# A two-layer encoder on one core: later block ends, later memory keys, and four more row-tile pairs in seven products

## The chip, the cores and the metric

The kernel runs on one core of a Trainium2 chip. The metric is the device time of one execution in microseconds; the time of a kernel is the median of its runs. The profile is one further execution under the hardware profiler. Engines are named as there: PE is the matrix engine (PEld its weight loads), DVE the vector engine, ACT the scalar engine, POOL the GpSimd engine, and SP the engine that issues most DMAs.

## What is computed

An encoder of two layers on one sequence of 256 tokens, model width 2048, all in float32:

```python
for l in range(DEPTH):                       # 2
    h = rmsnorm(x, norm_g[l])
    proj = h @ w_in[l]                       # 2048 x 7168: a_x a_b a_c a_g | d_q d_k d_v d_g | m_q m_g
    y_a = short_gated_conv(a_x, a_b, a_c, conv_w[l], conv_b[l]) * silu(a_g)        # 768 wide
    q, k = rmsnorm(d_q), rmsnorm(d_k)        # 6 heads x 2 halves x 64
    o_d = softmax(q1 k1 + alibi) v - lam * softmax(q2 k2 + alibi) v
    y_d = rmsnorm(o_d, g) * (1 - lam_init) * silu(d_g)                             # 768 wide
    mk, mv = split(rmsnorm(mem, mem_norm_g[l]) @ w_mem_kv[l])                      # 256 memory tokens
    y_m = softmax(rmsnorm(m_q) rmsnorm(mk)) mv * silu(m_g)                         # 512 wide, 4 heads
    x = x + concat(y_a, y_d, y_m) @ w_out[l]
```

## The kernel before, and what orders its work

**Products in three parts.** A float32 operand is split in two numbers, hi and lo: ACT rounds it (`hi`), DVE subtracts (`lo`). A product is three matmuls, hi x hi, hi x lo and lo x hi, each 128x512 (`products`, L278, and `product`, L325). Activations stand turned (features on partitions) as stationary tiles: `xT` for the input of a layer, `yT` for the mixed heads, `memT` for the memory. Weights stream: a chunk is two row tiles (256 rows) of 512 columns, loaded by SP into one of four `raw` buffers, split into one of four `hi` and one of four `lo` buffers (`load_w`, L263). 256 tokens are two token tiles, so a chunk is 2 x 2 x 3 = 12 matmuls.

**Blocks.** `block` (L286) makes 512 columns of a projection: eight chunks into two PSUM accumulators (there are four `acc` banks, so two blocks' worth). Layer 0 goes first through the memory's keys and values of both layers, then blocks 0 to 5 of the attention columns (0 to 2 are queries and keys, 3 to 5 values and gates), then the memory head's two blocks, then the convolution's six, then the output projection.

**Pairs in seven products.** Two neighbouring column blocks (near and far) and two row tiles make a 2x2 by 2x2 product, which `seven` (L345) computes with seven products in place of eight: the weights come in as two `wide` tiles of 1024 columns, DVE forms four differences, ACT and DVE split them; sums of the token tiles come from `token_sums` (L330). `joint` (L1033) runs a near block with some of its row tiles as pairs: it opens the far block's accumulators and four more banks `x1, x5, x6, x7`; the keys of `places` say before which row index a pair is emitted, `collect` adds the x banks up into `u`, and `gather` (L1066) adds the block's accumulators to them. Before, one pair is made in layer 0 (blocks 3 and 4, before index 10) and one in layer 1 (blocks 1 and 2, before index 8), besides those of the output projections.

**Ends of blocks.** After its last chunk a block's accumulators are read. For queries and keys that is `normed_steps` (L405): ACT squares groups of 64 columns with a sum (L413), POOL turns the sums into row factors (L414, L185, an ALU power), ACT multiplies each group by its factor (L421) into a sheet; then `qk_T` (L500) turns the sheet: a DVE transpose of 32x32 blocks (L451), a trip through DRAM (`carry`, L468 and L472, on SP) and a split into `yT`. Before, `normed` runs all of `normed_steps` at once, directly behind the block. Other ends are read by ACT and DVE in place: gates by `silu2`, values by a scaled copy, the convolution's inputs by `scaled`, `times` and `gate`.

**Memory keys.** `mem_keys` (L809) norms a layer's keys in the same way (groups of 128), and `keys` (L815) turns them: four DMAs out and one back on POOL's queue (L821, L822, `kd`), then a DVE transpose into `mkT` (L824), held in program order.

**What sets the order.** The program is written as one sequence with side tasks: `run_side` (L208) counts chunks and runs one step of each task that is due; `later(g, n)` (L191) makes a task due n chunks on, and a task's `yield n` puts its next step n chunks later. A scheduler then orders each engine's instructions by their readiness in its own estimate, except those wrapped in `keep_in_program_order` (`pin`), which keep the order in which they were emitted. Each engine works through its queue in order, so an instruction that waits holds up all behind it.

Of the kernel before, what the change touches and what calls it, by code (L numbers as in the profile page):

```python
# [40 lines left out]
BIG = 3.0e38  # L41

# [7 lines left out]
def encoder(ctx: ExitStack, tc: tile.TileContext, x, mem, norm_g, w_in, conv_w, conv_b,  # L50
# [354 lines left out]
    def normed_steps(acc, gs, st, home):  # L405

        ng, w = NB // gs, gs // B
        ss = small.tile([P, NT, ng], F32, tag=f"ss{ng}", name=nm("ss"))
        r = small.tile([P, NT, ng], F32, tag=f"rs{ng}", name=nm("rs"))
        for t in range(NT):  # L410
            for g in range(ng):
                sq = small.tile([P, gs], F32, tag="sq", name=nm("sq"), bufs=1)
                nc.scalar.activation(sq, acc[t][:, g * gs:(g + 1) * gs], AF.Square, accum_out=ss[:, t, g:g + 1])  # L413
            nc.gpsimd.tensor_scalar(ss[:, t], ss[:, t], 1.0 / gs, col(st, ET, t), ALU.mult, ALU.add)  # L414
            rsqrt(r[:, t], ss[:, t])
            yield 1
        both = home()
        for t in range(NT):
            for g in range(ng):
                j, b = divmod(g * w, NA)  # L420
                nc.scalar.activation(both[:, b:b + w, j, t], strips(acc[t][:, g * gs:(g + 1) * gs]), AF.Copy,  # L421
                                     scale=r[:, t, g:g + 1])
# [233 lines left out]

    def mem_pair(l, n, st):
        heads = (2 * n, 2 * n + 1)
        es = []
        for h in heads:  # L660
            while held["e"] == 2:
                yield 1
            held["e"] += 1
            es.append((yield from mem_scores(l, h, st)))
            yield 2
        yield 4
# [142 lines left out]
    def mem_keys(l, kraw):  # L809

        nat = yield from normed_steps([kraw[:, t] for t in range(NT)], P, stm[0], sheets("v"))
        yield 6
        yield from keys(l, nat)

    def keys(l, nat):  # L815


        d = dram.tile([NA, B, NA, W_MEM // P * NT * B], F32, name=nm("kd"))
        flat = nat.rearrange("p b j t c -> p b (j t c)")
        for a in range(NA):  # L820
            tc.keep_in_program_order(nc.gpsimd.dma_start(d[:, :, a].rearrange("b c r -> c b r"), flat[a * B:(a + 1) * B]))  # L821
        tc.keep_in_program_order(nc.gpsimd.dma_start(flat, d.rearrange("b c a r -> (b c) a r")))  # L822
        yield 8
        tc.keep_in_program_order(nc.vector.transpose(  # L824
            mkT[l].rearrange("p j (t a i) -> p (j t) a i", t=NT, a=NA),
            nat.rearrange("p a j t c -> p (j t) a c")))
# [5 lines left out]
    class Memory:  # L832
# [5 lines left out]
        def load(self, s):  # L838
            if s in self.raw or s in self.parts or s >= DEPTH * KT + KT // CK:
                return  # L840
            l, k = divmod(s, KT)
            self.raw[s] = raw_tile()
            if l == DEPTH:
                pin(nc.sync.dma_start(self.raw[s], x_row_tiles(w_in[0], k * CK)[:, :, C_D:C_D + NB]))
# [170 lines left out]
    for l in range(DEPTH):  # L1015
# [11 lines left out]
        def x_sums(n, tag):  # L1027
            home = keep.tile([P, 2, 4, P], F32R, tag=tag, name=nm("sums"))
            for _ in token_sums(xT, 2 * n, home):
                pass  # L1030
            return home

        def joint(b, places, summed, home):  # L1033
# [18 lines left out]
            def pair_at(n):  # L1052
                def run(near):
                    rows = lambda k: x_row_tiles(w_in[l], k, 1)[:, 0, C_D + b * NB:C_D + (b + 2) * NB]
                    seven(xT, 2 * n, summed[n], rows, near, far, x, n == 0, n == len(places) - 1,
                          ((tmp, ("sh", "e")[n]),) * 2, lambda: None, ((tmp, "e"), (keep, "mga"))[l])
# [6 lines left out]
                    between={c: pair_at(n) for n, c in enumerate(places)})  # L1063
# [13 lines left out]
        near_b, far_b, places, tags, home = ((3, 4, (10,), ("bgx",), "bgT"), (1, 2, (8,), ("bgT",), "bgx"))[l]  # L1077
        far, summed = None, []
        for b in order:
            if l == 0 and b == near_b - 1:  # L1080
                summed = [x_sums(n, tags[n]) for n in range(len(places))]
            if b in begun:
                acc = x_block([(C_D + b * NB, NB)], ALLK[-QT:], acc=begun[b])
                if b == 3:
                    for n in range(len(places)):
                        summed.append(x_sums(n, tags[n]))
            elif b == near_b:
                acc, far, us = joint(b, places, summed, home)
                acc = gather(acc, us[0:2])
            elif b == far_b:  # L1090
                acc = x_block([(C_D + b * NB, NB)], ALLK[2 * len(places):], acc=far, opened=(True, False))
                acc = gather(acc, us[2:4])
            else:
                acc = x_block([(C_D + b * NB, NB)], ready=m.ready if l == 0 and b == order[0] else None)
# [10 lines left out]
            if b < 3:  # L1105
                tasks.append(later(qk_T(l, yT, normed(acc, HALF, st, sheets(("mqT", "mga", "e")[b])),
                                 (0, 0, 4) if b == 0 else (0, 4, 2) if b == 1 else None,
                                 (256, 0, 2) if b == 1 else (0, 2, 4) if b == 2 else None), 8))
            else:
                for t in range(NT):  # L1110
                    if b == 3:
                        nc.scalar.activation(v[:, t, 0:NB], acc[t], AF.Copy, scale=col(st, R, t))
                    elif b == 4:
                        nc.scalar.activation(v[:, t, NB:768], acc[t][:, 0:256], AF.Copy, scale=col(st, R, t))
                        silu2(ga[:, t, 0:256], acc[t][:, 256:512], st, t)
                    else:
                        silu2(ga[:, t, 256:768], acc[t], st, t)
# [5 lines left out]
        def turn_mq(nat):  # L1123
# [4 lines left out]
        tasks.append(later(turn_mq(normed(acc, P, st, sheets("bgx"))), 8))  # L1128
        acc = x_block([(C_M + W_MEM, NB)])
        for t in range(NT):  # L1130
            a = tmp.tile([P, NB], F32, tag="nat", name=nm("a"), bufs=3)
            silu2(a, acc[t], st, t)
            tc.keep_in_program_order(nc.vector.transpose(mga[:, :, :, t], a.rearrange("p (j b c) -> p b j c", b=NA, c=B)))
# [62 lines left out]
        acc = x_block([(C_B, NB)])  # L1196
        scaled(both_rows(bg, 0, 4), acc, HR2)
        acc = x_block([(C_B + NB, 256), (C_G + NB, 256)])
        scaled(both_rows(bg, 4, 6), [a[:, 0:256] for a in acc], HR2)
        gate(NB, 256, [a[:, 256:512] for a in acc])  # L1200
        acc = x_block([(C_G, NB)])
        gate(0, NB, acc)
        tasks.append(later(turn_bg(list(range(CG))), 9))
        acc = x_block([(C_X, NB)])
        ux = sheet(tmp, "e")
        scaled(both_rows(ux, 0, 4), acc, R2)
        acc = x_block([(C_C, NB)])
        times(both_rows(ux, 0, 4), acc)
# [12 lines left out]
        acc = x_block([(C_X + NB, 256), (C_C + NB, 256)])  # L1221
        ux = sheet(tmp, "yn", 2)
        scaled(both_rows(ux, 0, 2), [a[:, 0:256] for a in acc], R2)
        times(both_rows(ux, 0, 2), [a[:, 256:512] for a in acc])
        tasks.append(later(conv([4, 5], ux, wait=3), 4))
# [110 lines left out]
```

## Time and profile before

| | us |
|---|---|
| median of 3 runs (lowest, highest) | 918.17 (917.14, 918.65) |
| profiled execution | 920.46 |
| span of its instructions | 918.7 |
| PE busy | 910.9 |
| DVE busy | 638.8 |
| ACT busy | 589.0 |
| POOL busy | 125.3 |

The granted clock of PE was 1.0 of full speed. In the rows that follow, a group of instructions reads: line, engine, operation, output<-inputs (buffer numbers left out), shape, count, then busy us and mean ns, then the idle time of the engine before them and what ended it. A timeline row reads: start us, duration us, engine, line, operation; in brackets the idle time before it and its releaser. Line numbers are those of the kernel before.

### The profile page before, as it was taken

What the parts mean: (1) busy time and instruction counts of PE and PEld (TensorE: products, weight loads), DVE (VectorE), ACT (ScalarE), POOL (GpSimd) and SP (SyncE); (2) the same over time, 40 slices, a digit from 0 to 9 for tenths busy, and PEclk for the clock granted to TensorE, in tenths of its full rate; (3) what the DMA queues carried; (4) which work ended last, traced back from release to release, by engine and by line L of the source; (5) the groups of instructions that cost most, each with busy time, mean ns of one, the idle gap of its engine ahead of it and who ended that gap; (6) DMA issues with size and microseconds to landing.
All of it is one profiled execution on the core that took longest, in us unless ns stands there. A gap on an engine that the chain in (4) does not pass through costs nothing.

```text
span 918.7 us, 12662 instructions
## 1 busy us (share of the span) xinstructions
PE 910.9 (99%) x4203; PEld 752.3 (82%) x4203; DVE 638.8 (70%) x877; ACT 589.0 (64%) x1226; POOL 125.3 (14%) x187
## 2 busy tenths in 40 slices
PE   9999999999999999999999999999999999999998
PEld 6887787888888888888888888888888888888887
DVE  5557645677658658677689666667658678588786
ACT  6679776757767656545557558787667666546352
POOL 2376142200031010000000202221032010000000
PEclk9999999999999999999999999999999999999999
DMA  8898777876777989978776874988768998968842
GB/s 288 284 266 252 236 227 226 255 215 221 222 212 205 256 228 262 265 234 246 254 228 226 259 251 130 277 241 238 223 183 230 266 271 248 271 206 241 281 154 92
DMA packets 244051, 215.18 MB, mean 234 GB/s; under 512 B 131977, under 2 KB 171721, under 8 KB 243985
## 3 DMA queue, kind: packets, MB, share of 16 engines
q1 hardware_dynamic: 239008, 208.71, 76.1%
q0 software_dynamic: 3776, 4.59, 1.9%
q10 hardware_dynamic: 1200, 1.07, 0.3%
q8 instruction: 33, 0.54, 0.2%
q14 instruction: 34, 0.27, 0.1%
HBM read 193.30 MB, written 21.00 MB: 233 GB/s over the span
## 4 chain that ended last, share of the span: by engine, by line
PE 88%; DMA 5%; ACT 2%; DVE 2%; POOL 2%; issue 1%; DVEq 0%; ACTq 0%; POOLq 0%
PE acc L282 80%; PE x L328 2%; DMA raw<-in_w_mem_kv_dram 2%; DMA raw<-in_w_in_dram 2%; PE acc L328 2%; PE po L489 1%; PE s L579 1%; DMA sh<-kd 1%; DVE lo L869 1%; PE po L706 1%; DVE xf L743 1%; ACT hi L271 1%; ACT sq L413 1%; POOL rs L185 1%; ACT sh L421 0%
## 5 line engine op out<-in xcount | busy, mean ns | idle before, releaser
L282 PE MATMUL acc<-hi,xT 128*128 128x512 f32 x1760 | 550.4, 390 | 0.0
L272 DVE TENSOR_TENSOR lo<-raw,hi 128x1024 fp32r<-128x1024 f32 x266 | 323.6, 1221 | 171.0 <-ACT hi L271 166.1
L271 ACT CAST hi<-raw 128x1024 fp32r<-128x1024 f32 x266 | 278.4, 1052 | 189.0 <-PE acc L282 138.2
L282 PEld LDWEIGHTS acc<-hi,xT 128*128 128x128 f32 x1760 | 330.3, 188 | 68.6
L282 PE MATMUL acc<-lo,xT 128*128 128x512 f32 x880 | 343.1, 390 | 2.0 <-DVE lo L272 1.6
L282 PEld LDWEIGHTS acc<-lo,xT 128*128 128x128 f32 x880 | 165.2, 188 | 36.3 <-DVE lo L272 2.0
L282 PE MATMUL acc<-hi,yT 128*128 128x512 f32 (+1 forms) x432 | 134.2, 388 | 0.0
L282 PEld LDWEIGHTS acc<-hi,yT 128*128 128x128 f32 x432 | 81.0, 188 | 16.7
L282 PE MATMUL acc<-lo,yT 128*128 128x512 f32 x216 | 83.7, 388 | 0.0
L282 PE MATMUL acc<-hi,memT 128*128 128x512 f32 x248 | 78.7, 393 | 0.0
L869 DVE SCALAR_TENSOR_TENSOR lo<-raw,cva,hi 128x1024 fp32r<-128x1024 f32 (+1 forms) x34 | 40.7, 1218 | 24.8 <-ACT hi L868 24.8
L282 PEld LDWEIGHTS acc<-hi,memT 128*128 128x128 f32 x248 | 46.1, 188 | 9.5
L282 PE MATMUL acc<-lo,memT 128*128 128x512 f32 x124 | 48.6, 392 | 0.7 <-DVE lo L869 0.7
L282 PEld LDWEIGHTS acc<-lo,yT 128*128 128x128 f32 x216 | 40.6, 188 | 8.4
L868 ACT ACTIVATE hi<-raw,cva 128x1024 fp32r<-128x1024 f32 (+1 forms) x34 | 36.5, 1098 | 7.6 <-DMA raw<-in_w_mem_kv_dram 7.0
L354 ACT CAST hi<-wide 128x1024 fp32r<-128x1024 f32 x21 | 22.0, 1056 | 18.1 <-DVE wide L357 7.4
L185 POOL TENSOR_TENSOR rs<-ss,root 128x8 f32<-128x8 f32 (+1 forms) x20 | 31.7, 1583 | 1.7
L354 DVE TENSOR_TENSOR lo<-wide,hi 128x1024 fp32r<-128x1024 f32 x21 | 25.4, 1221 | 8.4 <-ACT hi L354 8.2
L414 POOL TENSOR_SCALAR ss<-ss,st 128x8 f32<-128x8 f32 (+1 forms) x16 | 10.5, 654 | 137.4 <-ACT sq L413 137.4
L282 PEld LDWEIGHTS acc<-lo,memT 128*128 128x128 f32 x124 | 23.3, 188 | 6.6 <-DVE lo L869 1.8
L596 ACT ACTIVATE e<-e,mx 128x256 f32<-128x256 f32 x48 | 23.8, 497 | 6.7 <-DVE mx L591 6.0
L394 POOL TENSOR_SCALAR stt<-ssum 128x2 f32<-128x2 f32 x3 | 1.5, 507 | 187.3 <-DVE ssum L770 187.3
(207 smaller groups left out, 858.6 us busy)
## 6 DMA issues: line engine op xcount, KB each, us to landing
raw<-in_w_in_dram SPq DMA_DIRECT2D x188, 512.0 KB, 4.9
raw<-in_w_out_dram SPq DMA_DIRECT2D x54, 512.0 KB, 4.6
raw<-in_w_in_dram SPq DMA_DIRECT2D x64, 256.0 KB, 4.1
raw<-in_w_mem_kv_dram SPq DMA_DIRECT2D x30, 512.0 KB, 6.1
d<-sh SPq DMA_DIRECT2D x88, 128.0 KB, 4.4
sh<-d SPq DMA_DIRECT2D x72, 128.0 KB, 3.8
wide<-in_w_out_dram SPq DMA_DIRECT2D x10, 512.0 KB, 5.9
xs<-in_x_dram SPq DMA_DIRECT2D x4, 512.0 KB, 6.5
```

Of the source, the lines that this page charges most:

```text
L185: nc.gpsimd.tensor_tensor(r, t, root[:, 0:n], ALU.pow)
L271: nc.scalar.copy(hi, raw)
L272: nc.vector.tensor_tensor(lo_, raw, hi.bitcast(F32), ALU.subtract)
L282: i = nc.tensor.matmul(acc, left, right, start=start, stop=stop)
L328: nc.tensor.matmul(acc, left[a], right[b], start=first and i == 0, stop=last and i == 2)
L354: return ((hi, pin(nc.scalar.copy(hi, src))), (lo, pin(nc.vector.tensor_tensor(lo, src, hi.bitcast(F32), ALU.subtract))))
L413: nc.scalar.activation(sq, acc[t][:, g * gs:(g + 1) * gs], AF.Square, accum_out=ss[:, t, g:g + 1])
L414: nc.gpsimd.tensor_scalar(ss[:, t], ss[:, t], 1.0 / gs, col(st, ET, t), ALU.mult, ALU.add)
L489: nc.tensor.matmul(po[:, t, :], eT[:, i, t, k, :], v[:, k, h * P:(h + 1) * P], start=k == 0, stop=k == NT - 1)
L596: nc.scalar.activation(e[:, c, i], e[:, c, i], AF.Exp, bias=mx[:, c, i:i + 1], scale=-1.0, accum_out=sm[:, c, i:i + 1])
L868: both = (nc.scalar.activation(hi[:, j], raw[:, j], AF.Copy, scale=g), nc.vector.scalar_tensor_tensor(lo[:, j], raw[:, j], g, hi[:, j].bit ...
L869: nc.vector.scalar_tensor_tensor(lo[:, j], raw[:, j], g, hi[:, j].bitcast(F32), ALU.mult, ALU.subtract))
```

## The change

1. **Ends later.** `LAG = 2`. The end of every layer block becomes a task that is due two chunks after the block: `leave` for values and gates, `soon(...)` for the memory gate and the convolution, and `qk_T` and `turn_mq` now run `normed_steps` themselves, step by step, due after 2 chunks where the finished sheet was due after 8.
2. **The norm in one instruction a token tile.** The ACT multiplies by group (L421 before) become a DVE multiply of 128x512 by a broadcast factor, one for each token tile; squares yield after every fourth group.
3. **Later memory keys.** `keys` yields 11 chunks in place of 8 before its transpose; layer 0's sheet lies in another buffer.
4. **More pairs.** In layer 0 blocks 1 and 2, and 3 and 4, have two pairs each; in layer 1 blocks 1 and 2 have two. Token sums are made by a task (`all_x_sums`) and lie in `yT`'s last row tiles.
5. Memory pairs wait for the one before to have begun its scores.

```diff
+LAG = 2
+    def soon(what):
+        def once():
+            what()
+            yield
+        tasks.append(later(once(), LAG))
...
                 nc.scalar.activation(sq, acc[t][:, g * gs:(g + 1) * gs], AF.Square, accum_out=ss[:, t, g:g + 1])
+                if g % 4 == 3 and g + 1 < ng:
+                    yield 1
...
         for t in range(NT):
-            for g in range(ng):
-                j, b = divmod(g * w, NA)
-                nc.scalar.activation(both[:, b:b + w, j, t], strips(acc[t][:, g * gs:(g + 1) * gs]), AF.Copy,
-                                     scale=r[:, t, g:g + 1])
-            yield 1
+            to = both[:, :, :, t].rearrange("p (g b) j c -> p j g b c", b=w)
+            of = acc[t].rearrange("p (j g b c) -> p j g b c", g=NA // w, b=w, c=B)
+            nc.vector.tensor_tensor(to, of, r[:, t].rearrange("p (j g) -> p j g", g=NA // w).unsqueeze(3).unsqueeze(4)
+                                    .to_broadcast([P, NB // P, NA // w, w, B]), ALU.mult)
+            yield 2
...
-        nat = yield from normed_steps([kraw[:, t] for t in range(NT)], P, stm[0], sheets("v"))
-        yield 6
+        nat = yield from normed_steps([kraw[:, t] for t in range(NT)], P, stm[0], sheets(("bgT", "v")[l]))
+        yield 5
...
         tc.keep_in_program_order(nc.gpsimd.dma_start(flat, d.rearrange("b c a r -> (b c) a r")))
-        yield 8
+        yield 11
...
-        near_b, far_b, places, tags, home = ((3, 4, (10,), ("bgx",), "bgT"), (1, 2, (8,), ("bgT",), "bgx"))[l]
+        turned, raw, late = ((tmp, "sh"),) * 2, ((tmp, "e"),) * 2, ((keep, "v"), (keep, "ga"))
+        mga, bgx = (keep, "mga"), (keep, "bgx")
+        joints = ({1: ((4, 8), (turned, raw), (mga,) * 2, "bgT"), 3: ((6, 10), (late, turned), (bgx,) * 2, "bgT")} if l == 0
+                  else {1: ((6, 10), (raw, turned), (mga,) * 2, "bgx")})
...
-                acc = gather(acc, us[0:2])
+                finish = us[0:2]
...
+            def sums_of(acc=acc, us=finish):
+                return gather(acc, us) if us else acc
...
-                tasks.append(later(qk_T(l, yT, normed(acc, HALF, st, sheets(("mqT", "mga", "e")[b])),
+                tasks.append(later(qk_T(l, yT, sums_of, st, sheets(("mqT", "mga", "e")[b]),
                                  (0, 0, 4) if b == 0 else (0, 4, 2) if b == 1 else None,
-                                 (256, 0, 2) if b == 1 else (0, 2, 4) if b == 2 else None), 8))
+                                 (256, 0, 2) if b == 1 else (0, 2, 4) if b == 2 else None), 2))
...
-        acc = x_block([(C_B, NB)])
-        scaled(both_rows(bg, 0, 4), acc, HR2)
+        acc_b = x_block([(C_B, NB)])
+        soon(lambda: scaled(both_rows(bg, 0, 4), acc_b, HR2))
```

More of the change, by code (lines that the diff above doesn't have):

```diff
@@ L41 @@
 BIG = 3.0e38
+LAG = 2
+FIRST = 0
 C_X, C_B, C_C, C_G = 0, 768, 1536, 2304
@@ L655, in encoder @@
     spare, yTs, gates, summed_heads = {}, {}, {}, set()
+    begun_pairs = set()
     def mem_pair(l, n, st):
         heads = (2 * n, 2 * n + 1)
+        while n > 0 and (l, n - 1) not in begun_pairs:
+            yield 1
         es = []
@@ L665, in mem_pair @@
             yield 2
+        begun_pairs.add((l, n))
         yield 4
@@ L1025, in x_block, with x_sums, joint @@
             return block(xT, w_in[l], cols, order, rows=x_row_tiles, **how)
[L1027 to L1033, printed above, removed]
+        def x_sums(n):
+            home = yT[:, :, KT - QT + 2 * n:KT - QT + 2 * (n + 1)].rearrange("p two k (h r) -> p two (k h) r", r=P)
+            summed.append(home)
+            yield from token_sums(xT, 2 * n, home)
+        def joint(b, places, homes, singles, home, **how):
             near, far = accumulators(), accumulators()
@@ L1084, in encoder @@
                 if b == 3:
[L1085 to L1088, printed above, removed]
-                acc = gather(acc, us[0:2])
-            elif b == far_b:
+                    tasks.append(later(all_x_sums(), 1))
+            elif b in joints:
+                places = joints[b][0]
+                acc, far, us = joint(b, *joints[b])
+                finish = us[0:2]
+            elif b - 1 in joints:
                 acc = x_block([(C_D + b * NB, NB)], ALLK[2 * len(places):], acc=far, opened=(True, False))
-                acc = gather(acc, us[2:4])
+                finish = us[2:4]
             else:
-                acc = x_block([(C_D + b * NB, NB)], ready=m.ready if l == 0 and b == order[0] else None)
+                acc = x_block([(C_D + b * NB, NB)], ready=m.ready if l == 0 and b == 0 else None)
+            def sums_of(acc=acc, us=finish):
+                return gather(acc, us) if us else acc
             if b == 3:
@@ L1220, in encoder, with last_inputs @@
         tasks.append(later(all_sums(l, yT, sums), 1))
[L1221 to L1225, printed above, removed]
+        acc_xc = x_block([(C_X + NB, 256), (C_C + NB, 256)])
+        ux2 = sheet(tmp, "yn", 2)
+        def last_inputs():
+            scaled(both_rows(ux2, 0, 2), part(acc_xc, 0, 256), R2)
+            times(both_rows(ux2, 0, 2), part(acc_xc, 256, 256))
+        soon(last_inputs)
+        tasks.append(later(conv([4, 5], ux2, wait=3), 4))
         if l + 1 < DEPTH:
```

85 lines of the change are left out of this document (48 added, 37 removed).

## The prediction

> **What bounds the kernel now.** I read the page first: the busy shares, then the chain that ended last.
>
> ```profile
> span 918.7 us, 12662 instructions
> PE 910.9 (99%) x4203; PEld 752.3 (82%) x4203; DVE 638.8 (70%) x877; ACT 589.0 (64%) x1226; POOL 125.3 (14%) x187
> PE 88%; DMA 5%; ACT 2%; DVE 2%; POOL 2%; issue 1%; DVEq 0%; ACTq 0%; POOLq 0%
> ```
>
> PE is busy all the time, and 88% of the chain is PE. A busy PE need not be a PE at its rate, so I took the rate from one long piece of the chain, and then what PE waited for (line waited for: us in total, times, longest).
>
> ```profile
> 810.72 65.32 PE acc L282 x288
> PE acc L282 <- DVE lo L272: 1.6, 1, 1.6
> PE acc L282 <- DVE lo L861: 0.5, 1, 0.5
> ```
>
> 288 products of 128x512 in 65.32 us are 0.2268 us each, back to back: the stationary loads are hidden. This is the price of a product that is removed anywhere on the chain. PE's own waits are few; the two above are the largest behind weight splits. The timeline of PE gives their full size, start to start:
>
> ```profile
> 100.99 0.84 PE L282 MATMUL acc<-hi,xT 128*128 128x512 f32 x3
> 102.29 0.50 PE L282 MATMUL acc<-lo,xT 128*128 128x512 f32 x1 [0.46 <-DVE lo L861]
> 104.47 0.84 PE L282 MATMUL acc<-hi,xT 128*128 128x512 f32 x3
> 105.33 0.50 PE L282 MATMUL acc<-lo,xT 128*128 128x512 f32 x1
> 148.31 0.61 PE L282 MATMUL acc<-hi,xT 128*128 128x512 f32 x2
> 150.48 0.50 PE L282 MATMUL acc<-lo,xT 128*128 128x512 f32 x1 [1.56 <-DVE lo L272]
> ```
>
> Three products from 100.99 should be followed at 101.67 and are followed at 102.29: 0.62 us lost. In the same way 105.33 - 105.15 = 0.18, and 150.48 - 148.76 = 1.72. Together 2.52 us, all in layer 0's first two blocks. What DVE did instead of the split that PE wanted:
>
> ```profile
> 99.88 1.25 DVE L824 STREAM_TRANSPOSE mkT<-sh 128x1024 f32<-128x1024 f32 x1 [4.76 <-DMA sh<-kd]
> 147.87 1.25 DVE L824 STREAM_TRANSPOSE mkT<-sh 128x1024 f32<-128x1024 f32 x1 [6.38 <-DMA sh<-kd]
> 149.22 1.21 DVE L272 TENSOR_TENSOR lo<-raw,hi 128x1024 fp32r<-128x1024 f32 x1
> 139.81 0.57 POOL L822 DMA_DIRECT2D sh<-kd  x1 [4.66 <-DVE lo L272]
> ```
>
> DVE stood 4.76 and 6.38 us before the transposes of the memory keys, which are held in program order and wait for a DMA (the second one's read was issued by POOL at 139.81 and landed 8 us later); the splits are queued behind them.
>
> **Term 1, products.** A pair in seven products runs 7 x 3 = 21 matmuls in place of 24. In the input projections two pairs become six, so 4 x 3 = 12 matmuls of 128x512 go (the built programs differ by just that: 4163 and 4151 PE instructions). All stand on the chain: 12 x 0.2268 = **-2.72 us**.
>
> **Term 2, the keys' waits.** On DVE, around the transpose for layer 1's keys (mkT_115; lo are weight splits, sums the token sums of the pair), before:
>
> ```order
> L339 TENSOR_TENSOR sums_1459<-sums_1459,f_1457 128x128
> L824 STREAM_TRANSPOSE mkT_115<-sh_1078 128x1024
> L340 TENSOR_TENSOR sums_1459<-f_1457,sums_1459 128x128
> L272 TENSOR_TENSOR lo_1508<-raw_1505,hi_1507 128x1024
> L272 TENSOR_TENSOR lo_1526<-raw_1523,hi_1525 128x1024
> ```
>
> and now (u are the pairs' collected sums, rs the row factors of block 1):
>
> ```order
> L1075 TENSOR_TENSOR u_1207<-acc_1200,u_1207 128x512
> L280 TENSOR_TENSOR lo_1563<-raw_1560,hi_1562 128x1024
> L280 TENSOR_TENSOR lo_1591<-raw_1588,hi_1590 128x1024
> L832 STREAM_TRANSPOSE mkT_115<-sh_1074 128x1024
> L431 TENSOR_TENSOR sh_1607<-u_1207,rs_1497 128x4x4x32
> L280 TENSOR_TENSOR lo_1622<-raw_1619,hi_1621 128x1024
> ```
>
> The transpose stood ahead of block 2's splits and stands behind the last of them, three or four chunks (8 to 11 us) later. Its read is issued earlier besides: on POOL it now stands right behind block 0's first row factors, which fall into the first joint. Layer 0's transpose now has five more splits and a 2 us strip transpose ahead of it, 5 x 1.2 + 2 = 8 us, against the 4.76 us that it waited. So I take both waits as gone: **-2.52 us**; the bounds are 0 (they wait as long at the new place) and -2.52. On POOL, block 0's second row factors are queued behind the keys' read, which waits for the keys' four writes to land; those are issued while block 0 still runs, so I count nothing for it.
>
> **Term 3, what the joints cost.** The rows that price it (DVE, ACT, then the DMA view):
>
> ```profile
> L354 DVE TENSOR_TENSOR lo<-wide,hi 128x1024 fp32r<-128x1024 f32 x21 | 25.4, 1221 | 8.4 <-ACT hi L354 8.2
> L357 DVE TENSOR_TENSOR wide<-wide 128x512 f32<-128x512 f32 x14 | 9.7, 692 | 0.5
> L1068 DVE TENSOR_TENSOR u<-acc,u 128x512 f32<-128x512 f32 x8 | 5.2, 675 | 0.0
> L354 ACT CAST one<-wide 128x512 fp32r<-128x512 f32 x7 | 4.4, 627 | 0.3 <-DMA wide<-in_w_out_dram 0.3
> L451 DVE STREAM_TRANSPOSE sh<-sh 128x1024 f32<-128x1024 f32 x10 | 12.4, 1239 | 3.9 <-ACT sh L421 3.9
> L421 ACT ACTIVATE sh<-acc,rs 128x64 f32<-128x64 f32 x64 | 14.5, 335 | 5.0 <-POOL rs L185 5.0
> wide<-in_w_in_dram SPq DMA_DIRECT2D x4, 512.0 KB, 6.1
> 118.96 1.99 ACT L271 CAST hi<-raw 128x1024 fp32r<-128x1024 f32 x2
> 123.80 0.22 ACT L413 ACTIVATE sq<-acc 128x64 f32<-128x64 f32 x1
> 124.15 0.23 ACT L413 ACTIVATE sq<-acc 128x64 f32<-128x64 f32 x1
> 124.50 0.22 ACT L413 ACTIVATE sq<-acc 128x64 f32<-128x64 f32 x1
> 124.56 0.28 POOL L414 TENSOR_SCALAR ss<-ss,st 128x8 f32<-128x8 f32 x1 [6.83 <-ACT sq L413]
> 124.93 1.64 POOL L185 TENSOR_TENSOR rs<-ss,root 128x8 f32<-128x8 f32 x1
> 176.95 1.18 POOL L414 TENSOR_SCALAR ss<-ss,st 128x8 f32<-128x8 f32 x1 [5.07 <-ACT sq L413]
> 178.21 2.00 POOL L185 TENSOR_TENSOR rs<-ss,root 128x8 f32<-128x8 f32 x1
> ```
>
> A pair's DVE work is three splits, one half split and four differences: 3 x 1.22 + 0.7 + 4 x 0.69 = 7.1 us against 21 x 0.2268 = 4.8 us of PE. It is paid out of the lead that splits have over PE: four hi/lo buffers, so up to four chunks of 12 matmuls, 2.72 us each. The 128 ACT multiplies of the norm (64 of them took 14.5 us) become 20 on DVE; the trace has no such multiply with a broadcast factor, so I price it between 0.68 (the nearest row, a 128x512 add out of PSUM, L1068) and 1.24 us (a 128x1024 transpose), and take 0.68. Away from joints all this has cover: DVE gains 20 x 0.68 + 4 x 7.1, loses 8 splits of 1.22, and gains some 10 us of adds and token sums: from 639 to about 680 us of 915.
>
> In the first joint (layer 0, block 1) the cover is thin, since block 0's end now falls into the first pair. ACT (sq are squares of block 0's accumulators acc_1041 or acc_1035, sh its norm) before, right after block 0:
>
> ```order
> L271 CAST hi_1270<-raw_1268 128x1024
> L271 CAST hi_1294<-raw_1292 128x1024
> L413 ACTIVATE sq_1195,ss_1193<-acc_1041 128x64
> ...
> L271 CAST hi_1348<-raw_1346 128x1024
> ...
> L421 ACTIVATE sh_1231<-acc_1042,rs_1194 128x2x32 x8
> ```
>
> and now (one and hi of wide are the pair's casts):
>
> ```order
> L421 ACTIVATE sq_1253,ss_1245<-acc_1035 128x64
> L362 CAST one_1259<-wide_1255 128x512
> L362 CAST hi_1264<-wide_1256 128x1024
> L421 ACTIVATE sq_1305,ss_1245<-acc_1035 128x64
> ...
> L362 CAST hi_1270<-wide_1255 128x1024
> L421 ACTIVATE sq_1337,ss_1245<-acc_1036 128x64
> ...
> L362 CAST one_1373<-wide_1369 128x512
> L362 CAST hi_1274<-wide_1256 128x1024
> ```
>
> Sixteen squares now stand among the pair's casts, in batches of 4, 6 and 6, and the first waits for block 0's last matmul. From the start of that matmul: 0.39 until it ends, then squares at 0.35 (rows above), casts at 0.95 (two in 1.99), a half cast at 0.55 (estimate from 0.627 less the overlap that the casts show): 0.39 + 1.40 + 0.55 + 0.95 + 2.10 + 0.95 + 2.10 + 0.55 + 1.05 = 10.0 us until hi_1274 is there. In the built order PE has 40 matmuls from there to its first use: 40 x 0.2268 = 9.1. PE loses 0.9 to 1.0 us. DVE's multiplies (L431) wait for POOL, 2.1 us after the last square; the first ends at 4.7 + 2.1 + 0.7 = 7.5, and the difference behind it at 8.2, before ACT asks for it at 9.0.
>
> In layer 0's third block the same place is bound by DVE. Before, the pair's rows stand together:
>
> ```order
> L354 TENSOR_TENSOR one_1789<-wide_1785,one_1789 128x512
> L357 TENSOR_TENSOR wide_1785<-wide_1785 128x512
> ...
> L354 TENSOR_TENSOR lo_1801<-wide_1785,hi_1800 128x1024
> L354 TENSOR_TENSOR lo_1805<-wide_1786,hi_1804 128x1024
> L272 TENSOR_TENSOR lo_1835<-raw_1832,hi_1834 128x1024
> ```
>
> and now block 2's end is threaded through them:
>
> ```order
> L1075 TENSOR_TENSOR u_1208<-acc_1202,u_1208 128x512
> L362 TENSOR_TENSOR one_1711<-wide_1707,one_1711 128x512
> ...
> L362 TENSOR_TENSOR lo_1723<-wide_1707,hi_1722 128x1024
> L431 TENSOR_TENSOR sh_1806<-u_1208,rs_1664 128x4x4x32
> L362 TENSOR_TENSOR lo_1727<-wide_1708,hi_1726 128x1024
> L453 STREAM_TRANSPOSE sh_1607<-sh_1607 128x1024
> L280 TENSOR_TENSOR lo_1763<-raw_1760,hi_1762 128x1024
> ```
>
> From the last matmul of the accumulator that is gathered first: 0.39 + 0.68 (L1075) + 16 squares 5.6 + casts 0.55 + 0.95 + 0.95 + POOL 2.1 + multiply 0.68 + split 1.2 + transpose 1.2 + split 1.2 = 15.5 us to lo_1763; PE has 65 matmuls until it, 14.7 us. Loss 0.8. Layer 1's joint has its first pair after three chunks, one more than the first joint, and no such transpose inside; I put 0.2 there. Sum **+2.0 us**; bounds 0 (each chain 1 us shorter) and 5.3 (rival 1).
>
> The other ends move with a bank to spare: accumulators are used again eight chunks (21.8 us) later, so two chunks of lag leave 16 us for four or five instructions. The wide loads of the third joint stand behind four sheet reads on SP, about 8 us ahead of need, for 6.1 us: covered.
>
> **The sum.** -2.72 - 2.52 + 2.0 = -3.2 us. The profiled execution took 920.46 us (span 918.7), 2.3 above the median of 918.17; -3.2 gives 917.2 for it and **915.0** for the median. What can be told from no change is about 0.2%, 1.84 us.
>
> **Rivals.**
> 1. *The banks hold PE* (chance 0.12). In a joint the far accumulator takes the bank of the block before, which is now freed only by the first DVE multiply. PE comes to the far product after 36 matmuls, at 8.2; the multiply ends at 7.5. With POOL's long rows (1.18 + 2.00, 3.4 with the gaps) and the multiply at 1.24 it ends at 4.7 + 3.4 + 1.2 = 9.3, 1.1 late, and all behind it moves by as much: 3.3 us in three joints, -3.2 + 3.3 = +0.1, 918.3, no change. The rows from 124.56 speak against it, those from 176.95 for it. The Trainium skill, PSUM — Partial Sum Buffer, Summary: rules for kernel authors, says to evacuate promptly since PSUM is tight; by that rule the lag is itself the mistake. No row of this trace shows PE waiting for a bank.
> 2. *The keys still make DVE wait* (0.08), only later: term 2 is 0, -2.72 + 2.0 = -0.7, 917.5. Against it: 6.38 us is short beside the distance moved.
> 3. *The ends starve the pairs* (0.10), slower. With the same long rows at the second factors too: in the first joint the last square ends at 8.5, the factors are there at 11.9, and the second multiply, behind the split of hi_1274, ends at 13.6; the next raw split (lo_1318) is done at 14.8. PE wants it after 53 matmuls, 12.0: 2.8 us lost, in three joints 8.4: -5.24 + 8.4 = +3.2, 921.4. It decides from 2.4 us a joint on (7.1 in all). For it: every link, ACT to POOL to DVE to ACT, is serial. Against it: most POOL rows are short, and a loss in PE lets the rest catch up.
>
> **How the numbers follow.** The forecast, with joint losses from 0 to 3.4, has 0.70: 912.9 to 916.3. Rivals 1 and 2 make "same", 0.20; rival 3 "slower", 0.10. The range takes the forecast's and most of rivals 1 and 2: 912.5 to 917.6.
>
> **What would show it.** Right: 12 fewer matmuls; no wait of DVE for sh<-kd; no PE gap near 101 and 148; PE gaps near 1 us in the first pair of blocks 1 and 3 of layer 0, behind ACT and DVE; DVE near 680 us. Wrong: PE gaps over 2 us in each joint (rival 3), PE released by a multiply (rival 1), or a keys' transpose that still waits while PE stands (rival 2).

## The result, and the profile after

The changed kernel takes 922.62 us (median of 4 runs, 922.37 to 922.90) beside 917.78 us (4 runs, 917.14 to 918.65) for the kernel before: a ratio of 1.0052, 95% interval 1.0035 to 1.0070. It is slower, where 915.0 was forecast. Beside later experiments it took 922.71 against 919.20 (27 runs): 1.0036, 1.0023 to 1.0049. The changed kernel repeats within 1.3 us; the kernel before scatters, from 916.5 to 921.4 in 69 runs, and that turns out to matter. Two executions that ran far slower, one of the kernel before (1138 us) and the profiled one of the old pairs (1010 us, at a granted clock of 0.85), are left out of all that follows.

The page of the changed kernel, its span, busy time and chain by engine:

```profile
span 921.0 us, 12582 instructions
PE 910.5 (99%) x4191; PEld 751.0 (82%) x4191; DVE 678.3 (74%) x941; ACT 567.9 (62%) x1109; POOL 124.6 (14%) x187
PE 90%; ACT 3%; POOL 2%; DVE 2%; issue 2%; DMA 1%; SPq 0%; DVEq 0%; ACTq 0%; POOLq 0%
```

12 fewer matmuls (the page counted 4203 before; the prediction's 4163 and 4151 are counts of the built programs, with the same difference), and DVE at the 680 us that were forecast. Yet the span is 2.3 us longer. PE's waits name the lines (us in total, times, longest):

```profile
PE acc L336 <- DVE lo L362: 2.1, 2, 1.5
PE acc L290 <- DVE lo L280: 1.7, 2, 1.3
PE acc L336 <- ACT hi L362: 1.0, 2, 0.6
PE acc L336 <- DVE sh L431: 0.3, 1, 0.3
```

All four lie in the three joints (L336 is a pair's product, L362 its splits, L280 a raw chunk's split, L431 the new norm multiply). PE's timeline there:

```profile
127.16 0.40 PE L336 MATMUL acc<-hi,xT 128*128 128x512 f32 x1
127.89 0.51 PE L336 MATMUL acc<-hi,yT 128*128 128x512 f32 x1 [0.33 <-DVE sh L431]
129.57 0.50 PE L336 MATMUL acc<-hi,xT 128*128 128x512 f32 x1 [0.47 <-ACT hi L362]
134.22 0.50 PE L290 MATMUL acc<-lo,xT 128*128 128x512 f32 x1 [1.31 <-DVE lo L280]
176.80 0.50 PE L336 MATMUL acc<-hi,xT 128*128 128x512 f32 x1 [0.56 <-ACT hi L362]
180.15 0.50 PE L336 MATMUL acc<-lo,xT 128*128 128x512 f32 x1 [1.47 <-DVE lo L362]
182.42 0.50 PE L290 MATMUL acc<-lo,xT 128*128 128x512 f32 x1 [0.36 <-DVE lo L280]
566.31 0.50 PE L336 MATMUL acc<-lo,xT 128*128 128x512 f32 x1 [0.67 <-DVE lo L362]
```

Start to start, less the 0.23 us of a matmul, the gaps are 127.89 - 127.16 - 0.23 = 0.50, and in the same way 0.64 and 1.57 in the first joint (2.7 together); 0.72, 1.64 and 0.53 in block 3 of layer 0 (2.9); 0.83 and 0.25 in layer 1 (1.1). Sum 6.7. The matmuls around them follow each other at up to 0.24 us; counted against the 0.2268 us of the long stretch, PE loses 7.8 us in the joints in all. (The expectations below say 7.6.) The gaps at 101, 105 and 148 us are gone, and no wait of DVE for sh<-kd is left.

Why the splits are late, the rows of DVE and POOL in the first joint show (L424 and L187 are POOL's two steps from the sums of squares to the row factors, L830 its read of the memory keys):

```profile
123.64 1.22 DVE L362 TENSOR_TENSOR lo<-wide,hi 128x1024 fp32r<-128x1024 f32 x1
123.86 1.15 POOL L424 TENSOR_SCALAR ss<-ss,st 128x8 f32<-128x8 f32 x1 [5.84 <-ACT sq L421]
124.89 0.69 DVE L365 TENSOR_TENSOR wide<-wide,wide 128x512 f32<-128x512 f32 x1
125.08 2.03 POOL L187 TENSOR_TENSOR rs<-ss,root 128x8 f32<-128x8 f32 x1
127.15 0.69 DVE L431 TENSOR_TENSOR sh<-acc,rs 128x512 f32<-128x512 f32 x1 [1.56 <-POOL rs L187]
127.08 0.63 POOL L830 DMA_DIRECT2D sh<-kd  x1
127.81 1.82 POOL L424 TENSOR_SCALAR ss<-ss,st 128x8 f32<-128x8 f32 x1
128.35 2.42 DVE L362 TENSOR_TENSOR lo<-wide,hi 128x1024 fp32r<-128x1024 f32 x2
129.72 2.59 POOL L187 TENSOR_TENSOR rs<-ss,root 128x8 f32<-128x8 f32 x1
132.34 0.69 DVE L431 TENSOR_TENSOR sh<-acc,rs 128x512 f32<-128x512 f32 x1 [1.57 <-POOL rs L187]
132.95 1.22 DVE L280 TENSOR_TENSOR lo<-raw,hi 128x1024 fp32r<-128x1024 f32 x1
169.70 0.27 POOL L424 TENSOR_SCALAR ss<-ss,st 128x8 f32<-128x8 f32 x1 [5.67 <-ACT sq L421]
170.06 1.64 POOL L187 TENSOR_TENSOR rs<-ss,root 128x8 f32<-128x8 f32 x1
```

The last two rows are POOL's steps where they begin while DVE stands: 0.27 and 1.64 us. In the joint the same steps take 1.15 and 2.03, then 1.82 and 2.59 us. The long ones end at a fixed distance behind an instruction of DVE: the scale steps 0.07 to 0.15 us after a split's end (125.01 after 124.86; 129.63 after about 129.56), the powers 1.5 us after one (127.11 after 125.58; 132.31 after about 130.8). So DVE's splits and differences hold POOL up, and then DVE, in order, stands 1.56 and 1.57 us before the multiply that needs POOL's result, with the raw split that PE wants at 132.66 queued behind it. In the whole kernel that wait is one row of DVE's waits:

```profile
DVE sh L431 <- POOL rs L187: 18.3, 16, 1.9
```

The Trainium skill, SBUF — State Buffer, "Who interferes with whom", states the rule: a DVE instruction with two SBUF inputs contends with a GpSimd instruction that reads SBUF. The rows agree: every one of these splits and differences has two inputs in SBUF, and POOL's steps take up to 1.82 and 2.59 us beside them for 0.27 and 1.64.

### The profile page after: what moved, and what is told of

Read it like the earlier page. It is cut to its first block, busy times and chain, and to the rows that moved or that the text cites. A ratio compares the mean times of both kernels' runs of the same rounds, so it can differ in the third digit from the quotient of the medians.

```text
span 921.0 us, 12582 instructions
## 1 busy us (share of the span) xinstructions
PE 910.5 (99%) x4191; PEld 751.0 (82%) x4191; DVE 678.3 (74%) x941; ACT 567.9 (62%) x1109; POOL 124.6 (14%) x187
## 4 chain that ended last, share of the span: by engine, by line
PE 90%; ACT 3%; POOL 2%; DVE 2%; issue 2%; DMA 1%; SPq 0%; DVEq 0%; ACTq 0%; POOLq 0%
PE acc L290 81%; PE x L336 2%; ACT sq L421 2%; PE acc L336 2%; POOL rs L187 1%; PE po L491 1%; PE s L582 1%; POOL ss L424 1%; DMA raw<-in_w_in_dram 1%; DVE lo L280 1%; PE po L714 1%; PE acc L894 1%; ACT hi L362 1%; PE pt L728 0%; DMA raw<-in_w_mem_kv_dram 0%
## 5 line engine op out<-in xcount | busy, mean ns | idle before, releaser
L290 PE MATMUL acc<-hi,xT 128*128 128x512 f32 x1696 | 531.9, 390 | 0.0
L280 DVE TENSOR_TENSOR lo<-raw,hi 128x1024 fp32r<-128x1024 f32 x258 | 314.0, 1222 | 131.9 <-ACT hi L279 128.9
L279 ACT CAST hi<-raw 128x1024 fp32r<-128x1024 f32 x258 | 269.6, 1050 | 202.8 <-PE acc L290 167.0
L290 PEld LDWEIGHTS acc<-hi,xT 128*128 128x128 f32 x1696 | 318.4, 188 | 66.2
L290 PE MATMUL acc<-lo,xT 128*128 128x512 f32 x848 | 330.8, 390 | 1.7 <-DVE lo L280 1.7
L290 PEld LDWEIGHTS acc<-lo,xT 128*128 128x128 f32 x848 | 159.3, 188 | 34.6 <-DVE lo L280 2.9
L362 ACT CAST hi<-wide 128x1024 fp32r<-128x1024 f32 x33 | 34.4, 1048 | 39.4 <-DVE wide L365 28.5
L362 DVE TENSOR_TENSOR lo<-wide,hi 128x1024 fp32r<-128x1024 f32 x33 | 40.1, 1220 | 4.0 <-ACT hi L362 3.7
L187 POOL TENSOR_TENSOR rs<-ss,root 128x8 f32<-128x8 f32 (+1 forms) x20 | 32.9, 1643 | 1.7
L424 POOL TENSOR_SCALAR ss<-ss,st 128x8 f32<-128x8 f32 (+1 forms) x16 | 13.4, 837 | 130.2 <-ACT sq L421 130.1
```

Source lines behind the costliest of these rows:

```text
L187: nc.gpsimd.tensor_tensor(r, t, root[:, 0:n], ALU.pow)
L279: nc.scalar.copy(hi, raw)
L280: nc.vector.tensor_tensor(lo_, raw, hi.bitcast(F32), ALU.subtract)
L290: i = nc.tensor.matmul(acc, left, right, start=start, stop=stop)
L362: return ((hi, pin(nc.scalar.copy(hi, src))), (lo, pin(nc.vector.tensor_tensor(lo, src, hi.bitcast(F32), ALU.subtract))))
```

## The experiments

**Theory A**: POOL computes the row factors while the pair's splits run, is held up by them, and DVE then stands in the middle of the pair. **Rival B**: ACT is late with the pair's casts, since squares stand among them. **Rival C**: a pair's DVE work alone uses up the lead of the splits. Later, **rival D**: moving an end or a pair changes nothing, since the scheduler moves both.

| run | median us (runs) | ratio to before, 95% | PE gaps in the three joints, us |
|---|---|---|---|
| changed, again | 922.71 (5) | 1.0036 (1.0023 to 1.0049) | 2.7, 2.9, 1.1 |
| factors not waited for | 916.13 (5) | 0.9967 (0.9954 to 0.9979) | 0.5, 0, 0 |
| pairs later | 921.84 (6) | 1.0031 (1.0019 to 1.0043) | 1.0, 4.0 (slow matmuls behind the gap included), 1.6 |
| old key delays | 921.23 (8) | 1.0022 (1.0012 to 1.0032) | 1.1, 2.9, 1.1 |
| ends at once | 919.22 (11) | 0.9998 (0.9989 to 1.0006) | 0, 3.1, 0.5 |
| old pairs | 917.92 (11) | 0.9986 (0.9977 to 0.9995) | left out |
| before, late keys only | 918.72 (11) | 0.9992 (0.9983 to 1.0001) | |
| one step on POOL | 919.83 (11) | 1.0012 (1.0000 to 1.0023) | 1.0, 1.0, 1.0 |
| ends at once, one step | 916.95 (11) | 0.9981 (0.9972 to 0.9991) | 0, 1.9, 0 |
| ends at once, one pair in block 3 | 915.88 (7) | 0.9975 (0.9963 to 0.9988) | 0, 0.4, 0 |
| the same, one step | 915.37 (8) | 0.9969 (0.9958 to 0.9979) | 0, 0, 0 |

The kernel before took 919.39, 919.20 and 918.83 us beside the three sets; ratios are each to its own set (the first set is the factors, the later pairs and the old key delays; the third begins with one step on POOL). A difference in us from the changed kernel's 922.71, which belongs to the second set, holds up to 0.4 us of that shift.

### The kernel before, once more

No edit.

> The kernel before, unchanged, profiled once more. Its profiled execution was 2.3 us above the median of its other executions. If the three stalls of PE near 101, 105 and 148 us (2.52 us, in which DVE waits for the memory keys) belong to the program, they are there again with the same sizes and the time is near 920. If they depend on when the keys' DMAs land in one execution, they are smaller or gone and the time is near 918: then term 2 of the prediction counted a gain that the median does not hold.

918.58 us (one run). DVE's waits for the keys are shorter, and PE has no gap near 101, 105 or 148:

```profile
97.66 1.25 DVE L824 STREAM_TRANSPOSE mkT<-sh 128x1024 f32<-128x1024 f32 x1 [1.78 <-DMA sh<-kd]
144.95 1.25 DVE L824 STREAM_TRANSPOSE mkT<-sh 128x1024 f32<-128x1024 f32 x1 [4.48 <-DMA sh<-kd]
```

1.78 and 4.48 us in place of 4.76 and 6.38, and the lead of the splits covers that. Instead PE stands 0.90 us at 181.10, behind a cast of a `wide` tile. The stalls that the prediction priced do not come back in this execution; they are in one profile of two, and that execution was 2.3 us above the median: the two figures stood in the prediction side by side.

### The factors not waited for

```diff
-            nc.vector.tensor_tensor(to, of, r[:, t].rearrange(...
+            nc.vector.tensor_tensor(to, of, (root[:, 0:ng] if gs == HALF else r[:, t]).rearrange(...
```

> The changed kernel, but the norm multiplies of the query and key blocks (L431) take a constant column in place of the row factors; POOL still computes the factors, nobody reads them, and the output lacks that norm. Theory A (in the joints DVE stands behind the multiply that waits for POOL, with the pair's splits queued behind it): the waits of DVE on POOL there (18.3 us in the whole kernel) go, the PE losses of the joints fall from 7.6 us to 1 or less, 915.5 to 917. Rival B (ACT is late with the pair's casts, because the squares stand among them): little changes, 921 to 922.6. Rival C (a pair's 7.1 us of DVE beside 4.8 us of PE simply uses up the splits' lead): little changes either, 922 to 922.6.

916.13 us, 6.6 us under the 922.71 of the changed kernel. PE's waits in its profile, the first two at the start:

```profile
PE warm L131 <- DVE zeros L126: 1.2, 1, 1.2
PE acc L894 <- ACT hi L876: 0.5, 1, 0.5
PE acc L336 <- ACT hi L362: 0.4, 1, 0.4
```

Of eight gaps in the joints one is left, 0.53 us behind a cast at 129.5. The work is as it was, squares, casts and pairs, and POOL's steps for the second factors of block 2 still take 1.26 and 2.54 us; but nobody waits for them. ACT's order is all but the same (in block 3 one square moves behind a cast); on DVE the scheduler now puts both multiplies of block 2 ahead of the pair (from 165.86). So the run takes away the wait together with the place that the wait gives the multiplies. Theory A holds in this sense. Rival B is at most that one gap, and rival C shows no loss.

### The pairs later

```diff
-        joints = ({1: ((4, 8), ...), 3: ((6, 10), ...)} if l == 0 else {1: ((6, 10), ...)})
+        joints = ({1: ((8, 10), ...), 3: ((8, 10), ...)} if l == 0 else {1: ((8, 10), ...)})
```

> The changed kernel with the pairs of its three joints before row indices 8 and 10 in place of 4 and 8, 6 and 10, 6 and 10. The ends of the block before are then over when the first pair's splits begin, but the two pairs follow each other closely. Theory A (factors from POOL late inside the pair) and rival B (squares among the casts): the losses of 7.6 us fall to 2 or less, 916.5 to 918. Rival C (the pairs' DVE work alone): losses grow, since 14 us of DVE work now stand within two chunks, 924 or more.

921.84 us: a miss for theory A as I had written it, and for rival C, which asked for 924 or more. DVE still waits for POOL inside the pair of block 3 (L431 at 176.46, 1.53 us). All five waits of PE in the joints are now behind casts, but the longest cast (177.84) itself waited 3.64 us for a difference of DVE, which stands behind that multiply. The second pairs' gaps, 0.53 us in block 1 and 0.55 in layer 1, have no wait for POOL near them: there the pair's own work on DVE is what the cast waits for, a small piece of rival C. The pair's first split runs on DVE at 172.98, in the changed kernel at 172.94, so a later pair on PE still has its splits beside the end. What decides is where the two stand on DVE, not on PE. This run also shows a second price of a gap, told at the end.

### The old delays of the keys

```diff
-        yield 11
+        yield 8
```

(and 6 for 5 ahead of it)

> The changed kernel with the memory keys' delays as before (8 and 6 chunks in place of 11 and 5). If the later keys bring what term 2 says, the DVE waits ahead of the mkT transposes come back (about 5 and 6 us) and 2.5 us are lost: 925. If the gain was only in the profiled execution of the kernel before, or DVE has lead to spare here, the time stays at 922.6 within 0.7.

921.23 us, not 925, and below the other alternative too (922.6 within 0.7). The two intervals overlap (1.0012 to 1.0032 and 1.0023 to 1.0049), so the medians alone do not order the two. The profiles do for one gap: no wait of DVE for sh<-kd comes back, and the third gap of the first joint, 1.57 us, is not there. The rows of POOL and DVE there (L829 are the keys' writes):

```profile
126.05 2.00 POOL L187 TENSOR_TENSOR rs<-ss,root 128x8 f32<-128x8 f32 x1
128.00 2.29 POOL L829 DMA_DIRECT2D kd<-sh  x4
130.38 0.28 POOL L424 TENSOR_SCALAR ss<-ss,st 128x8 f32<-128x8 f32 x1
130.73 2.51 POOL L187 TENSOR_TENSOR rs<-ss,root 128x8 f32<-128x8 f32 x1
131.64 2.35 DVE L280 TENSOR_TENSOR lo<-raw,hi 128x1024 fp32r<-128x1024 f32 x2
```

Here the keys' four writes stand between the two factors, and the second power ends as late as in the changed kernel (133.24 for 132.31, in an execution whose joint stands 0.94 us later: PE's first gap ends at 128.83 for 127.89). Yet PE has no third gap, since two raw splits stand ahead of the second multiply on DVE (from 131.64), where in the changed kernel they stand behind it. A factor that comes as late has another price by the multiply's place in DVE's order. So in this kernel the later keys bring no gain that shows, and go with the worse order; that POOL's read of the keys between the two factors is what makes the 1.57 us, which was my guess, isn't shown.

### The changed kernel, once more

No edit; it was run beside the next three.

> The changed kernel, unchanged, beside the three that follow: the base for all of them. 0.4 to 0.6 per cent slower than the kernel before, with the joints' losses of 7 to 8 us at the same places (after 127, 175 and 565 us). If its profile again shows the third loss of the first joint (1.6 us near 132), where POOL issues the keys' read between the two factor computations, that loss belongs to the program.

922.71 us, gaps of 2.7, 2.9 and 1.1 us at the same places, the third of the first joint 1.57 us again. They belong to the program.

### The ends at once

```diff
-                tasks.append(later(qk_T(l, yT, sums_of, st, sheets(("mqT", "mga", "e")[b]),
+                steps = normed_steps(sums_of(), HALF, st, sheets(("mqT", "mga", "e")[b]))
+                tasks.append(later(qk_T(l, yT, at_once(steps),
...
-                                 (256, 0, 2) if b == 1 else (0, 2, 4) if b == 2 else None), 2))
+                                 (256, 0, 2) if b == 1 else (0, 2, 4) if b == 2 else None), 8))
```

(`at_once` runs all steps of the end directly behind the block; the other ends keep their lag.)

> The changed kernel with the ends of the query and key blocks emitted directly behind their block, as before, and not two chunks later; the pairs stay. Theory A, as it stands now (POOL computes the factors while the pair's splits run on DVE, is held up by them, and DVE then waits for POOL in the middle of the pair): the factors are asked for up to 5 us earlier, ahead of most of the splits; the joints lose 2 to 4 us in place of 7.6: 918 to 920.5 where the changed kernel has 923. Rival C (the pairs' DVE work alone): the losses stay, 922.5 to 923.5. Rival D (the scheduler puts the pair's work as early as its buffers allow, so both move together): the losses stay as well, and the waits of DVE on POOL too.

919.22 us, 3.5 us under the changed kernel and level with the kernel before. The first joint has both its pairs and no gap. DVE's and POOL's rows there:

```profile
126.93 0.69 DVE L431 TENSOR_TENSOR sh<-acc,rs 128x512 f32<-128x512 f32 x1 [1.81 <-POOL rs L187]
127.11 0.28 POOL L424 TENSOR_SCALAR ss<-ss,st 128x8 f32<-128x8 f32 x1 [0.21 <-ACT sq L421]
127.47 1.64 POOL L187 TENSOR_TENSOR rs<-ss,root 128x8 f32<-128x8 f32 x1
129.81 0.69 DVE L431 TENSOR_TENSOR sh<-acc,rs 128x512 f32<-128x512 f32 x1
```

The first wait is as long as ever (1.81), but the second factors' steps run unhindered, 0.28 and 1.64 us, and the second multiply waits for nothing. This is against rival C and rival D for the first joint. Block 3 is not helped, 3.1 us: there both of POOL's scale steps are held (1.68 and 2.12 us) and the multiplies wait 1.81 and 1.53 us.

### The old pairs

```diff
-        joints = ({1: ((4, 8), ...), 3: ((6, 10), ...)} if l == 0 else {1: ((6, 10), ...)})
+        joints = ({3: ((10,), (late,), (bgx,), "bgT")} if l == 0 else {1: ((8,), (raw,), (mga,), "bgx")})
```

(and token sums for one pair in place of two)

> The changed kernel with the pairs as before: one before index 10 in layer 0's block 3, one before index 8 in layer 1's block 1. 12 matmuls come back (+2.7 us); the first joint is gone and with it 2.7 to 3.1 us of loss, and the other two have one pair. Theory A: the one pair that is left still lies beside an end, so its loss stays in part (1 to 3 us in block 3, 0 to 1 in layer 1): 920 to 923. Rival C: with one pair a joint the lead is not used up and the losses go altogether: 918 to 918.5.

917.92 us, 4.8 us under the changed kernel although 12 matmuls (2.7 us) are back: some 7.5 us of losses left with the four pairs, about the 7.8 us that PE lost in the joints. By the numbers that is rival C's side of the expectation (918 to 918.5), but the run before shows that two pairs in the first joint cost nothing where the ends come earlier. In that joint the pairs cost only together with the late ends.

### The kernel before with late keys alone

```diff
-        yield 8
+        yield 11
```

(and layer 0's sheet and the 5 chunks ahead of it, as in the change)

> The kernel before with only the memory keys' delays of the change (11 and 5 chunks, layer 0's sheet in its other buffer). If the keys' waits cost the kernel before 2.5 us in every execution, it gains 2.5 us (0.27 per cent). If they cost that only in some executions, it gains 0 to 1 us in the median, and its times scatter less than those of the kernel before (917.7 to 921.3 in 13 runs).

918.72 us, 0.9992 (0.9983 to 1.0001): a gain of 0.5 us, from 1.6 to nothing by the interval, and not 2.5. Its scatter, 917.3 to 919.8 in 11 runs, is a little less. The wait for sh<-kd fell to 0.6 us in its profile, from 11 in that of the prediction. The wait went, and hardly any time with it.

### One step on POOL

```diff
-            nc.gpsimd.tensor_scalar(ss[:, t], ss[:, t], 1.0 / gs, col(st, ET, t), ALU.mult, ALU.add)
+            nc.scalar.activation(ss[:, t], ss[:, t], AF.Identity, scale=1.0 / gs, bias=col(st, ET, t))
```

> The changed kernel with the first of POOL's two steps for the factors (scale and epsilon, L424) as one ACT instruction of 128x8 behind the last square; POOL keeps the power alone. Theory A (POOL's chain, stretched by the pair's splits, is what DVE waits for): 0.3 to 1.9 us fall out of each chain, the DVE waits on POOL fall from 18 us to 8 to 12, and the joints lose 3 to 5 us in place of 7.6: 918.5 to 921 where the changed kernel has 922.7. Rival B (ACT's order decides): four more ACT instructions a joint, 922.7 to 924.

919.83 us, 2.9 us under the changed kernel (2.5 when each is taken against the kernel before beside it), with its lag and all its pairs. The gaps fell from 6.7 to 3.1 us, and the waits on POOL from 18.3:

```profile
DVE sh L431 <- POOL rs L187: 11.3, 13, 1.5
```

A shorter chain on POOL takes half the loss. The sum of these waits is not itself the loss: it is 20.0 us with the ends at once and 16.9 with one pair in block 3 besides, where the gaps sum to 3.6 and 0.4. What counts is whether a split that PE needs soon stands behind the wait. Four more ACT instructions a joint cost nothing that shows, against rival B.

### Ends at once and one step on POOL

Both edits.

> The query and key ends directly behind their blocks, all pairs of the change, and the step on ACT as in the run before. With the ends at once alone the time was 919.2, 3.1 us of it lost in the joint of layer 0's block 3. Theory A: a shorter chain takes 1 to 2 us off that loss: 917 to 918.5. If that joint is held by something other than POOL (the sums of block 2, which need the pair before collected, or DVE's own work): 919 to 919.5.

916.95 us, 0.9981 (0.9972 to 0.9991): faster than before. In block 3 a gap of 1.9 us stays, now behind ACT:

```profile
172.16 0.25 ACT L421 ACTIVATE sq<-u 128x64 f32<-128x64 f32 x1
...
174.44 0.26 ACT L421 ACTIVATE sq<-u 128x64 f32<-128x64 f32 x1
174.70 1.03 ACT L362 CAST hi<-wide 128x1024 fp32r<-128x1024 f32 x1
175.63 0.30 ACT L424 ACTIVATE ss<-ss,st 128x8 f32<-128x8 f32 x1
```

Seven squares of 0.38 us each, start to start, stand ahead of the cast that PE waits for. Where POOL's chain is short, rival B is what comes next.

### One pair in block 3

```diff
-3: ((6, 10), (late, turned), (bgx,) * 2, "bgT")
+3: ((10,), (late,), (bgx,), "bgT")
```

on top of the ends at once, and then with the one step on POOL as well.

> The query and key ends directly behind their blocks; two pairs in layer 0's block 1 and in layer 1's block 1 as in the change, but one pair before index 10 in layer 0's block 3, as before. Put together from the runs: the first joint loses nothing with the ends at once, block 3 nothing with its one late pair; 3 matmuls come back (+0.7): 919.2 - 3.1 + 0.7 = 916.8, faster than the kernel before by 0.26 per cent. If the loss in block 3 comes from block 2's end and not from the pair beside it, it stays: 919.5 to 920.

> The kernel of the run before with the step on ACT: what is left of losses in the joints (0.5 us in layer 1) may go too. 916 to 916.8; if ACT's four added instructions a joint cost more than POOL's chain, 917 to 918.

915.88 us (0.9975, 0.9963 to 0.9988) and 915.37 us (0.9969, 0.9958 to 0.9979), both 0.6 to 0.9 us under what was expected (the kernel before beside them is 0.4 us faster too); their intervals overlap, so the step on ACT is not shown to help here. In the second, PE waits at the start alone; its chain by engine, and PE's waits:

```profile
PE 99%; ACT 0%; DVE 0%; issue 0%
```

```profile
PE warm L131 <- DVE zeros L126: 1.2, 1, 1.2
PE acc L900 <- ACT hi L882: 0.4, 1, 0.4
```

The chain is PE from end to end, with three pairs more than the kernel before has in front of its output projections. This version beats both: the kernel before by 0.31% (0.21 to 0.42), and the change by some 0.7% (0.9969 / 1.0036 = 0.993; with the two intervals about 0.991 to 0.995).

**Not tested.** Part 2 of the change moved the multiply from ACT to DVE, the engine whose work holds POOL up. In the profile of the kernel before it was ACT that waited for the factors (L421 for L185, 10.6 us in 9 waits), with casts queued behind it in place of splits. That could cost PE too: in the kernel before, once more, ACT stands 2.25 us before L421 at 178.37, the cast of a `wide` tile follows at 179.96, and PE then stands its 0.90 us. No run puts the multiply back on ACT with late ends and all the pairs, so how much of the loss comes with this part stays open.

## Why the prediction was wrong

- **Term 1, the products, -2.72 us**: right. Twelve matmuls went, and the runs with old and new pairs fit that price (7.5 us lost with the pairs, 7.8 us counted in the joints).
- **Term 2, the keys' waits, -2.52 us**: the waits went as forecast, the gain was mis-sized. It was read from one execution whose time was 2.3 us above the median, and then taken off the median. In another execution those gaps are not there, and late keys alone bring 0.5 us, not clear of nothing. That is about 2 us of the miss. The step that failed is the last one, "-3.2 gives 917.2 for it and 915.0 for the median": a stall behind a DMA in a run above the median may be the very thing that puts it there. That it was so in this run fits the second profile, 1.9 us shorter without those gaps, but two profiles do not prove it.
- **Term 3, the joints, +2.0 us**: the mechanism was in the right places, the size was not: 2.7, 2.9 and 1.1 us of gaps (6.7, and 7.8 in all with the slower matmuls around them) for 1.0, 0.8 and 0.2. This is the larger part of the miss, 5.8 us. The step that failed is "DVE's multiplies (L431) wait for POOL, 2.1 us after the last square". In the first joint the two steps took 3.25 us (123.86 to 127.11), and for the second factors 5.2 with the keys' read ahead of them (127.08 to 132.31). The sum for the first joint also followed the first multiply alone; the second, with the raw split queued behind it, stands in rival 3 only, and it cost 1.57 us. ACT's part, which I had as the bound there (0.9 to 1.0), is 0.5 with POOL's wait taken away.
- The prediction had the rows, and chose among them by number: "most POOL rows are short". It should have asked what DVE did beside each. In the trace of before the long rows stand beside a pair's work, and a short one beside an idle DVE:

```profile
176.77 1.22 DVE L354 TENSOR_TENSOR lo<-wide,hi 128x1024 fp32r<-128x1024 f32 x1
178.02 0.69 DVE L357 TENSOR_TENSOR wide<-wide,wide 128x512 f32<-128x512 f32 x1
122.90 1.23 DVE L272 TENSOR_TENSOR lo<-raw,hi 128x1024 fp32r<-128x1024 f32 x1 [0.51 <-ACT hi L271]
126.13 1.22 DVE L272 TENSOR_TENSOR lo<-raw,hi 128x1024 fp32r<-128x1024 f32 x1 [2.00 <-ACT hi L271]
```

  The 1.18 us step of 176.95 ends at 178.13, 0.14 after the first of these; the 2.00 us power ends at 180.21, 1.5 after the second. The 0.28 and 1.64 us steps of 124.56 and 124.93 began while DVE stood from 124.13 to 126.13. In a joint most of POOL's steps meet the pair's work, so the long rows were the rule for the place that was priced.
- **The rivals**: rival 3 came true, with a chance of 0.10: the ends starve the pairs, through POOL's long rows. Its price of 2.8 us a joint, 8.4 in all, stands beside 2.7, 2.9 and 1.1. That 2.8 meets 2.7 in the first joint is luck: only 1.57 us of it is the raw split behind the second multiply, the rest is rival 1's piece and a cast. Rival 1 is in it as a piece: 0.50 us in which PE waited for the multiply that frees the bank. Rival 2 did not occur. The rule of the Trainium skill that stands with rival 1 (PSUM — Partial Sum Buffer, Summary: rules for kernel authors: evacuate promptly) would have pointed the right way, though for another reason than a scarce bank: with prompt ends the first joint loses nothing (block 3 still loses 3.1 us).
- What I counted right: DVE's busy time (678 for 680 us) and the multiply (0.69 us for 0.68).

The sum by the runs: -2.7 for the products, about -0.5 for the keys, +7.8 in the joints, +4.6 together; measured were 3.5 and 4.8 us.

## What to carry to other kernels

Where a cross-engine chain is put among dense work of one engine, price its links from rows that stand beside such work, not from the commonest row. A stall that one profiled execution shows is worth its length only if that execution's time is near the median; if it is above, look for the stall in a second profile first. Work that delays a consumer is judged by its place in that engine's queue: a factor equally late cost PE 1.6 us or nothing, depending on whether the split that PE needed stood behind the multiply or ahead of it.

## What the runs showed of the hardware

**DVE holds POOL up.** A 128x8 scale step of POOL takes 0.27 us alone and, beside DVE instructions with two SBUF inputs, up to 1.82 us in the first joint of the changed kernel (2.12 at 176.87 in the run with the ends at once); a 128x8 power takes 1.64 alone and up to 2.59 there (2.69 at 558.42 in the run with one step on POOL). Only its start is held: once begun (127.47 in the run with the ends at once), a power of 1.64 us ran on through a split that started at 127.54, and the split kept its 1.22 us.

**A gap of PE can cost twice.** In the run with the pairs later PE stood 2.25 us, and the matmuls behind it followed each other at 0.43 us in place of 0.23. The columns of these windows are: stretch, us, busy time (count) of PE, PEld, DVE, ACT and POOL, granted clock, DMA share, GB/s.

```profile
170.00:176.00 6.00, 6.00 (x28) 4.99 (x27) 4.41 (x6) 3.71 (x11) 3.53 (x3) 1.00 0.79 284
176.00:179.00 3.00, 0.75 (x5) 0.29 (x3) 2.51 (x4) 1.16 (x2) 0.42 (x1) 0.96 0.03 9
179.00:182.00 3.00, 3.00 (x7) 2.42 (x8) 2.96 (x4) 2.30 (x3) 0.00 (x0) 0.50 0.00 0
182.00:188.00 6.00, 6.00 (x27) 4.89 (x26) 5.84 (x7) 3.01 (x4) 0.00 (x0) 0.99 0.88 175
```

The clock was 0.50 for some 3 us, which cost seven matmuls 0.2 us each, 1.4 us on top of the gap. A gap of 1.70 us, in the run with the ends at once and one step, had no such tail. The six executions of the run with the pairs later show a mean clock of 0.998, one of them 0.999: 3 us at half clock in 920 are 0.16%, so the drop seems to come back in most of them. The Trainium skill, TensorE: Matmul & The Clock Gate, Part 1, puts the drop to half clock behind an idle window of about 3.4 us; here it came behind 2.25 us without a matmul, and the measurement decides.
